# Mixer B's small matmuls in fewer lists: keys and values, outputs and output transposes each in one

## The chip, the core and the metric

One core of a Trainium2 chip runs the whole program. The metric is the device time of one execution in microseconds, median of three runs. On this core TensorE (PE) does the matmuls and transposes, with its weight loads (PEld) beside them; VectorE (DVE), ScalarE (ACT) and GpSimd (POOL) do the elementwise work; SyncE (SP) issues the transfers. Each engine takes its instructions strictly in the order of its own program, and waits on semaphores for the others.

## What is computed

Two layers over 1024 positions of width 1024, in fp32. Layer 0 mixes by dilated window attention, layer 1 by a gated linear recurrence (mixer B); behind each mixer stands a squared-ReLU MLP, and behind each of the four a residual sum with layer norm. The change lies in mixer B, with 8 heads of width 128 and chunks of 64 positions:

```python
q, key, log_f, v = chunks(q, K), chunks(key, K), chunks(log_f, K), chunks(v, V)
b = jnp.cumsum(log_f, axis=3)
q_dec = q * jnp.exp(b)
k_dec = key * jnp.exp(-b)
a = jnp.where(causal, jnp.einsum('bhcid,bhcjd->bhcij', q_dec, k_dec), 0.0)
o_intra = jnp.einsum('bhcij,bhcje->bhcie', a, v)
kv = jnp.einsum('bhcjd,bhcje->bhcde', key * jnp.exp(b_last - b), v)
def step(state, inp):
    dec, kv_c = inp
    return dec[..., None] * state + kv_c, state
_, states = lax.scan(step, s0, ...)
o_inter = jnp.einsum('bhcid,cbhde->bhcie', q_dec, states)
o = o_intra + o_inter
o = o * lax.rsqrt(jnp.mean(o * o, axis=-1, keepdims=True) + RMS_EPS) * norm_g
return o.reshape(B, S, H * V) @ w_out
```

## The kernel before

The kernel is written against a tile layer, which adds the semaphores and, within the limits that the code sets, puts each engine's instructions into an order at compile time. Every large matmul is three passes: fp32 operands are split into a high and a low part (`split`, L157 and L158; `wh`, `wl` for weights).

`hgrn` runs over 8 heads. A head has six **slots**, two halves of the positions for each of forget gate (t = 1), query (t = 0) and value (t = 2). Each slot projects with `proj` (L192 to L194, 24 matmuls of 128x512 into one of three PSUM banks "mm"), copies the bank with ScalarE (L1821), then takes one **list of pieces** from `pend` and runs it. Behind the slot in which both halves of a t are there stands that t's `gate` (L1765 to L1797): a chain over 128x1024 elements on ScalarE, VectorE and, for two additions (L1781 and L1795), GpSimd. The gates are those of the head being projected; the pieces are those of the head before, so both lie beside each other.

The pieces of a head come from `head_pieces`, which returns lists, one for each following slot:

- `trans` transposes values and keys on TensorE (L1677) into banks "pt"; ScalarE copies them (L1678) to `vn` and `k2n`.
- `amat(j)` makes the masked product of queries and keys of a half (L1685, banks "s"), and VectorE writes it to `aT` (L1687).
- `kv(j)` multiplies keys with values for eight (j = 0) or seven (j = 1) chunks (L1697, two banks), and VectorE steps the state through them (L1703, L1705): `stA` holds the states of the first half, `stB` of the second. A step reads the one before.
- `omat(j)` adds `aT` times values (L1718) and queries times states (L1723) into a bank, "o" for j = 0 and "s" for j = 1. Then the result is normalised: squares on ScalarE (L1726), a reduction (L1728) and small operations on VectorE (L1729 to L1735) with a logarithm and an exponential on ScalarE (L1730, L1731), and the scaled result `on` on VectorE (L1737).
- `otr(j)` transposes `on` (L1745), ScalarE copies it to `oN` with the norm's gain (L1746), and for heads 0 to 4 a transfer stores it.

A fp32 matmul of the pieces shows as two passes in the records, so `kv(0)` is 16 of them. Head 0's lists start one slot later. The last head's lists go to `outproj_ln`, whose `tick` counts its groups of three matmuls (L204 to L206) and hands out the lists evenly over 56 of them; what TensorE does there beside them is the output projection over the heads that are already done.

Of the kernel before, what the change touches and what calls it, by code (L numbers as in the profile page):

```python
# [69 lines left out]
def trunk_kernel(  # L70
# [32 lines left out]
    def U(name, dt=F32):  # L103
        return up.tile([P, 1024], dt, name=name, tag="u")

    def bank(tag, name):
        return ps.tile([P, 512], F32, name=name, tag=tag, bufs={"mm": 3, "s": 2, "pt": 2, "o": 1}[tag])

    def small(shape, name, bufs=4, dt=F32):
        return sp.tile(shape, dt, name=name, tag=name, bufs=bufs)  # L110
# [1548 lines left out]
    def hgrn(xs, late, consts, pre, gw):  # L1659
# [8 lines left out]
        def head_pieces(hd, kd, kd2, qd, vT, dec, oNt):  # L1668
            st = {}

            def trans(src, name):
                d = U(name)
                for j in range(2):
                    pt = bank("pt", "hpt")
                    for i in range(4):
                        b = j * 4 + i
                        nc.tensor.transpose(pt[:, i * P:(i + 1) * P], src[:, b * P:(b + 1) * P], ident)  # L1677
                    act(d[:, j * 512:(j + 1) * 512], pt, AF.Copy)  # L1678
                st[name] = d
# [9 lines left out]
            def kv(j):  # L1689
                if j == 0:  # L1690
                    st["S"] = [U("stA"), U("stB")]
                kb = [bank("s" if j else "pt", "kvps") for _ in range(2)]
                cs = [c for c in range(j * 8, j * 8 + 8) if c < NCH - 1]
                for c in cs:
                    r = slice((c % 2) * CH, (c % 2) * CH + CH)
                    t = c // 2
                    nc.tensor.matmul(kb[c % 2][:, (t % 4) * P:(t % 4 + 1) * P], st["k2n"][r, t * P:(t + 1) * P],  # L1697
                                     st["vn"][r, t * P:(t + 1) * P], start=True, stop=True, skip_group_check=True)
                for c in cs:
                    dst = state(c + 1)  # L1700
                    kvc = kb[c % 2][:, (c // 2 % 4) * P:(c // 2 % 4 + 1) * P]
                    if c == 0:
                        nc.vector.tensor_copy(dst, kvc)  # L1703
                    else:
                        nc.vector.scalar_tensor_tensor(dst, state(c), dec[:, c:c + 1], kvc,  # L1705
                                                       op0=ALU.mult, op1=ALU.add)

            def state(c):
                return st["S"][c // 8][:, (c % 8) * P:(c % 8 + 1) * P]

            def omat(j):
                o = bank("o" if j == 0 else "s", "ho")
                for i in range(4):
                    t = j * 4 + i
                    cs = slice(i * P, (i + 1) * P)
                    both = [(c, o[(c % 2) * CH:(c % 2) * CH + CH, cs]) for c in (2 * t, 2 * t + 1)]
                    for c, oc in both:
                        nc.tensor.matmul(oc, aTs[j][:, i * P + (c % 2) * CH:i * P + (c % 2) * CH + CH],  # L1718
                                         st["vn"][:, t * P:(t + 1) * P], start=True, stop=c == 0,
                                         skip_group_check=True)  # L1720
                    for c, oc in both:
                        if c:
                            nc.tensor.matmul(oc, qd[:, c * CH:(c + 1) * CH], state(c), start=False, stop=True,  # L1723
                                             skip_group_check=True)
                sq = wp.tile([P, 512], F32, name="sq", tag="p")
                act(sq, o, AF.Square)  # L1726
                w = small([P, 4, 4], "rms")
                nc.vector.tensor_reduce(w[:, 0], sq.rearrange("p (t e) -> p t e", e=P), axis=AX.X, op=ALU.add)  # L1728
                nc.vector.tensor_scalar(w[:, 0], w[:, 0], 1.0 / P, RMS_EPS, op0=ALU.mult, op1=ALU.add)  # L1729
                act(w[:, 1], w[:, 0], AF.Ln)  # L1730
                act(w[:, 1], w[:, 1], AF.Exp, scale=-0.5)  # L1731
                nc.vector.tensor_mul(w[:, 2], w[:, 0], w[:, 1])
                nc.vector.tensor_mul(w[:, 2], w[:, 2], w[:, 1])
                nc.vector.tensor_scalar(w[:, 2], w[:, 2], -0.5, 1.5, op0=ALU.mult, op1=ALU.add)
                nc.vector.tensor_mul(w[:, 3], w[:, 2], w[:, 1])  # L1735
                on = wp.tile([P, 512], F32, name="on", tag="pts", bufs=4)
                nc.vector.tensor_mul(on.rearrange("p (t e) -> p t e", e=P), o.rearrange("p (t e) -> p t e", e=P),  # L1737
                                     w[:, 3].unsqueeze(2).broadcast_to([P, 4, P]))
                st["on", j] = on

            def otr(j):
                on = st.pop(("on", j))
                pt = bank("o" if j else "pt", "opt")
                for i in range(4):
                    nc.tensor.transpose(pt[:, i * P:(i + 1) * P], on[:, i * P:(i + 1) * P], ident)  # L1745
                act(oNt[:, j * 512:(j + 1) * 512], pt, AF.Identity, scale=gT[:, hd:hd + 1])  # L1746
                if hd < SPILL[1] and j == 1:
                    nc.sync.dma_start(ond[1, hd], oNt)
# [2 lines left out]
            keys = lambda: trans(kd2, "k2n")  # L1751
            return [
                [lambda: trans(vT, "vn")] + (amats + [keys] if hd else [keys] + amats),
                [lambda: kv(0)],
                [lambda: omat(0), lambda: kv(1)],
                [lambda: omat(1)],
                [],
                [lambda: otr(0)],
                [lambda: otr(1)],
            ]  # L1760

        def gate(hd, t, e, cur, c):
# [40 lines left out]
        for hd in range(8):  # L1803
# [29 lines left out]
            oNt = U("oN")  # L1833
            oN.append(ond[1, hd] if hd < SPILL[1] else oNt)
            new = head_pieces(hd, cur["kd"], cur["kd2"], cur["qd"], e[2], cur["dec"], oNt)
            if hd == 0:
                new = [[]] + new
# [109 lines left out]
```

## Time and profile before

| | us |
|---|---|
| median of three runs | 2760.66 (2760.09 to 2762.2) |
| the profiled execution | 2761.49 |
| its span, first to last instruction | 2759.7 |
| stage of mixer B's projections | 1688 to 2035 |
| period of one head there (kv(0) to kv(0)) | 43.80 |

The profile is of one execution. Rows of a timeline are start in us, duration, engine, line, operation, output<-inputs, shapes and count, and in brackets how long the engine was idle before and what ended that. Matmuls overlap in the pipeline, so a duration is longer than the time to the next start; the starts tell what a matmul costs. A row of a stretch has its length, then busy time and count of TensorE, its weight loads, VectorE, ScalarE and GpSimd, the granted clock of TensorE (1.00 is full), the share of the DMA engines and GB/s. A row of waits has total, count and longest.

### The profile page before, as it was taken

The page shows a single profiled execution, that of the slowest core. Times are in us where ns is not written, and L with a number is a line of the kernel's source. Part 1 is how long each engine was busy: PE and PEld are TensorE (multiplying, and loading weights), DVE is VectorE, ACT ScalarE, POOL GpSimd, SP SyncE. Part 2 cuts the span into 40 slices and gives each one's busy share as a digit, 9 for nine tenths or more (in the row PEclk, how much of TensorE's full clock was granted, in tenths as well). Part 3 has the DMA queues.
Part 4 walks back from the last instruction along what each step waited for, and adds up shares of the span by engine and source line. Part 5 has one row for each costly group of instructions (what it writes and reads, how often), then busy time and mean ns, then how long its engine had stood idle before and what let it go on. Part 6 is the DMA issues. An engine that isn't in the chain of part 4 may idle for free.

```text
span 2759.7 us, 40110 instructions
## 1 busy us (share of the span) xinstructions
PE 2734.4 (99%) x14312; PEld 2237.2 (81%) x14312; DVE 2076.6 (75%) x3876; ACT 1419.4 (51%) x3059; POOL 69.0 (2%) x46
## 2 busy tenths in 40 slices
PE   9999999999999999999999999999999999999998
PEld 7888888888888777888888888888888888888887
DVE  8868877777888768876696777565678887678687
ACT  5555555555555456445454435455552545455443
POOL 0000000000000001000000000010100100000000
PEclk9999999999999999999999999999999999999999
DMA  8767666766767324454584852001142464485654
GB/s 303 257 209 214 197 205 191 234 185 212 225 208 226 120 94 160 168 211 152 186 290 134 275 171 92 31 32 62 65 130 104 149 220 170 143 292 191 217 176 129
DMA packets 204041, 485.02 MB, mean 176 GB/s; under 512 B 28992, under 2 KB 42816, under 8 KB 203840
## 3 DMA queue, kind: packets, MB, share of 16 engines
q1 hardware_dynamic: 203072, 482.19, 52.6%
q8 instruction: 113, 1.85, 0.3%
q14 instruction: 88, 0.72, 0.1%
q10 hardware_dynamic: 768, 0.26, 0.0%
HBM read 362.69 MB, written 94.11 MB: 166 GB/s over the span
## 4 chain that ended last, share of the span: by engine, by line
PE 92%; DVE 5%; ACT 1%; issue 1%; DMA 1%; SPq 0%; POOL 0%; DVEq 0%; ACTq 0%; POOLq 0%
PE pmm L752 8%; PE pmm L750 8%; PE pmm L751 8%; PE pup L1272 7%; PE pup L1270 7%; PE pup L1271 7%; PE pdy L1421 4%; PE pdy L1425 4%; PE pdy L1424 4%; PE pdx L1424 3%; PE pdx L1425 3%; PE pdx L1421 3%; PE pmm L192 3%; PE pmm L194 3%; PE pmm L193 3%; PE s L559 3%
## 5 line engine op out<-in xcount | busy, mean ns | idle before, releaser
L750 PE MATMUL pmm<-xh,H 128*128 128x512 f32 x1008 | 402.1, 399 | 2.0 <-ACT H L487 1.9
L752 PE MATMUL pmm<-xh,H 128*128 128x512 f32 x1008 | 394.0, 391 | 2.3 <-DVE H L495 2.2
L751 PE MATMUL pmm<-xl,H 128*128 128x512 f32 x1008 | 393.0, 390 | 0.7 <-DVE xl L158 0.7
L752 PEld LDWEIGHTS pmm<-xh,H 128*128 128x128 f32 x1008 | 189.2, 188 | 44.9 <-DVE H L495 4.3
L750 PEld LDWEIGHTS pmm<-xh,H 128*128 128x128 f32 x1008 | 189.5, 188 | 40.4 <-ACT H L487 3.0
L751 PEld LDWEIGHTS pmm<-xl,H 128*128 128x128 f32 x1008 | 189.7, 188 | 37.7 <-DVE xl L158 1.1
L575 ACT ACTIVATE p<-p,stats 128x128 f32<-128x128 f32 (+1 forms) x384 | 167.9, 440 | 81.6 <-DVE stats L572 81.4
L1421 PE MATMUL pdy<-dT,dS 128*128 128x512 f32 x512 | 199.2, 389 | 0.0
L1424 PE MATMUL pdy<-dT,dS 128*128 128x512 f32 x512 | 199.2, 389 | 0.0
L1425 PE MATMUL pdy<-dT,dS 128*128 128x512 f32 x512 | 199.2, 389 | 0.0
L572 DVE CUSTOM_DVE_ANT_0 p<-s,mask 128x128 f32<-128x128 f32 (+1 forms) x384 | 111.1, 348 | 98.9 <-PE s L559 91.0
L157 ACT ACTIVATE dS<-dr 128x512 fp32r<-128x512 f32 x192 | 119.4, 622 | 69.9 <-PE pdy L1425 36.2
L192 PE MATMUL pmm<-f0nh,wh 128*128 128x512 f32 x384 | 153.2, 399 | 0.0
L194 PE MATMUL pmm<-f0nh,wl 128*128 128x512 f32 x384 | 149.8, 390 | 0.0
L193 PE MATMUL pmm<-f0nl,wh 128*128 128x512 f32 x384 | 149.7, 390 | 0.0
L158 DVE TENSOR_TENSOR dS<-dr,dS 128x512 fp32r<-128x512 f32 x192 | 131.5, 685 | 7.6 <-ACT dS L157 7.6
L157 ACT ACTIVATE dT<-hold 128x512 fp32r<-128x512 f32 x128 | 80.1, 626 | 78.5 <-DVE hold L1400 33.4
L1231 ACT ACTIVATE H<-wc 128x512 fp32r<-128x512 f32 x128 | 77.2, 626 | 77.6 <-DVE wc L1224 46.4
L1425 PEld LDWEIGHTS pdy<-dT,dS 128*128 128x128 f32 x512 | 96.1, 188 | 20.1
L1424 PEld LDWEIGHTS pdy<-dT,dS 128*128 128x128 f32 x512 | 96.1, 188 | 19.9
L1421 PEld LDWEIGHTS pdy<-dT,dS 128*128 128x128 f32 x512 | 96.1, 188 | 19.8
L587 ACT ACTIVATE pts<-ppt 128x512 f32<-128x512 f32 (+1 forms) x146 | 77.7, 575 | 44.4 <-PE ppt L584 44.1
(412 smaller groups left out, 6836.0 us busy)
## 6 DMA issues: line engine op xcount, KB each, us to landing
xh<-xtd SPq DMA_DIRECT2D x110, 512.0 KB
xl<-xtd SPq DMA_DIRECT2D x110, 512.0 KB
dr<-hd SPq DMA_DIRECT2D x192, 256.0 KB
dr<-in_w_down_dram SPq DMA_DIRECT2D x128, 256.0 KB
rot<-e SPq DMA_DIRECT2D x192, 128.0 KB
wa<-in_w_up_dram SPq DMA_DIRECT2D x48, 512.0 KB
wb<-in_w_attn_dram SPq DMA_DIRECT2D x36, 512.0 KB
wa<-in_w_attn_dram SPq DMA_DIRECT2D x33, 512.0 KB
```

Source lines behind the costliest of these rows:

```text
L157: act(hi, raw, AF.Copy)
L192: nc.tensor.matmul(o, wh[:, k], xs.h(k), start=k == 0, stop=False)
L193: nc.tensor.matmul(o, wh[:, k], xs.l(k), start=False, stop=False)
L194: nc.tensor.matmul(o, wl[:, k], xs.h(k), start=False, stop=k == NK - 1)
L750: nc.tensor.matmul(o, wh, hi[k // 2][:, c], start=begin and k == 0, stop=False, skip_group_check=True)
L751: nc.tensor.matmul(o, wh, lo[k // 2][:, c], start=False, stop=False, skip_group_check=True)
L752: nc.tensor.matmul(o, wl, hi[k // 2][:, c], start=False, stop=end and k == 3, skip_group_check=True)
L1270: nc.tensor.matmul(o, wh, xf.h(b, k), start=begin and k == 0, stop=False, skip_group_check=True)
L1271: nc.tensor.matmul(o, wh, xf.l(b, k), start=False, stop=False, skip_group_check=True)
L1421: nc.tensor.matmul(o[q], h, T_[:, L], start=begin, stop=False, skip_group_check=True)
L1424: nc.tensor.matmul(o[q], h, T_[:, R], start=False, stop=False, skip_group_check=True)
L1425: nc.tensor.matmul(o[q], l, T_[:, L], start=False, stop=end, skip_group_check=True)
```

## The change

```diff
@@ -1751,12 +1751,11 @@
             keys = lambda: trans(kd2, "k2n")
             return [
                 [lambda: trans(vT, "vn")] + (amats + [keys] if hd else [keys] + amats),
-                [lambda: kv(0)],
-                [lambda: omat(0), lambda: kv(1)],
-                [lambda: omat(1)],
+                [lambda: kv(0), lambda: kv(1)],
                 [],
-                [lambda: otr(0)],
-                [lambda: otr(1)],
+                [lambda: omat(0), lambda: omat(1)],
+                [],
+                [lambda: otr(0), lambda: otr(1)],
             ]
```

Seven lists become six. `kv(1)` moves up one slot, `omat(0)` moves down one, `otr(1)` moves up one; `otr(0)`, `omat(1)` and `kv(0)` stay. Between `omat(1)` and `otr(1)` lie two slots instead of three, between `omat(0)` and `otr(0)` too. No instruction is added or removed. The order of SP's instructions is the same, and GpSimd's; on the other engines it differs only from the first head's pieces to the last head's. In the changed kernel each line behind the lists has a number lower by one.

In heads 1 to 5 TensorE's order follows the lists: 15 matmuls of kv in one row, two projections, 31 of omat in one row, two projections, eight output transposes, one projection, then the next head's transposes and masked products. Three places where the scheduler decides:

VectorE, a middle head, from the state steps to the first result, before (`kvps` are kv's banks, `stA` and `stB` the states, `ls` and `ze` the gate's tiles, a_ its scratch, `rms` the small tile of the normalisation, `sq` the squares):

```order
L1703 COPY stA<-kvps 128x128
L1705 SCALAR_TENSOR_TENSOR stA<-stA,dec,kvps 128x128 x6
L1705 SCALAR_TENSOR_TENSOR stB<-stA,dec,kvps 128x128
L1772 SCALAR_TENSOR_TENSOR ls<-ze,a_17383 128x1024
L1773 SCALAR_TENSOR_TENSOR ze<-ze,a_17383 128x1024
L1728 TENSOR_REDUCE rms<-sq 128x4
L1705 SCALAR_TENSOR_TENSOR stB<-stB,dec,kvps 128x128
```

and now:

```order
L1703 COPY stA<-kvps 128x128
L1705 SCALAR_TENSOR_TENSOR stA<-stA,dec,kvps 128x128 x6
L1705 SCALAR_TENSOR_TENSOR stB<-stA,dec,kvps 128x128
L1705 SCALAR_TENSOR_TENSOR stB<-stB,dec,kvps 128x128 x7
L1771 SCALAR_TENSOR_TENSOR ls<-ze,a_17399 128x1024
L1772 SCALAR_TENSOR_TENSOR ze<-ze,a_17399 128x1024
L1776 TENSOR_SCALAR ls<-ls,hc_C,hc_A 128x1024
L158 TENSOR_TENSOR wl<-wr,wh 128x1024
L1777 TENSOR_TENSOR ls<-ls,a_17399 128x1024
L1778 SCALAR_TENSOR_TENSOR a_17399<-smask,ls 128x1024
L1728 TENSOR_REDUCE rms<-sq 128x4
```

All state steps now stand ahead of the gate, and the first reduction of the outputs behind the gate's scan (L1779 before, L1778 now).

VectorE, a middle head, from the first result `on` to the second (`ho` is omat's bank, `qe` the query, `wl` the low part of a weight), before:

```order
L1737 TENSOR_TENSOR on<-ho,rms 128x512
L1784 TENSOR_TENSOR ze<-a_17032,ze 128x1024
L1728 TENSOR_REDUCE rms<-sq 128x4
L1794 SCALAR_TENSOR_TENSOR a_17185<-qe,a_17185 128x1024
L1729 TENSOR_SCALAR rms<-rms 128x4
L158 TENSOR_TENSOR wl<-wr,wh 128x1024
L1732 TENSOR_TENSOR rms<-rms 128x4
L1733 TENSOR_TENSOR rms<-rms 128x4
L1734 TENSOR_SCALAR rms<-rms 128x4
L1735 TENSOR_TENSOR rms<-rms 128x4
L1797 TENSOR_TENSOR qe<-qe,a_17185 128x1024
L1737 TENSOR_TENSOR on<-ho,rms 128x512
```

and now, from ahead of the first result to the second (ahead of these rows stand L1793, L1783, L1732 and L1728):

```order
L1733 TENSOR_TENSOR rms<-rms 128x4
L158 TENSOR_TENSOR wl<-wr,wh 128x1024
L1734 TENSOR_SCALAR rms<-rms 128x4
L1729 TENSOR_SCALAR rms<-rms 128x4
L1735 TENSOR_TENSOR rms<-rms 128x4
L1737 TENSOR_TENSOR on<-ho,rms 128x512
L1796 TENSOR_TENSOR qe<-qe,a_17536 128x1024
L1732 TENSOR_TENSOR rms<-rms 128x4
L1733 TENSOR_TENSOR rms<-rms 128x4
L1734 TENSOR_SCALAR rms<-rms 128x4
L1735 TENSOR_TENSOR rms<-rms 128x4
L1737 TENSOR_TENSOR on<-ho,rms 128x512
```

Before, the first result was done ahead of the gate's L1784, and of the second half only L1737 stood behind the query's last product L1797. Now both results come behind the gate (L1783), and the second half's small operations and its `on` behind the query's last product (L1796 now).

TensorE, head 7's pieces in the output projection (`hpt` are banks for transposes, `ho` omat's bank, `pmm` the output projection's), before:

```order
L1677 MATMUL hpt<-ident,ze 128x128 x4
L1718 MATMUL ho<-vn,aT 64x128
L1677 MATMUL hpt<-ident,ze 128x128 x4
L1697 MATMUL kvps<-vn,k2n 128x128 x8
L1718 MATMUL ho<-vn,aT 64x128
L1723 MATMUL ho<-stA,qe 64x128
L1718 MATMUL ho<-vn,aT 64x128 x2
L1697 MATMUL kvps<-vn,k2n 128x128 x3
L1723 MATMUL ho<-stA,qe 64x128
L1697 MATMUL kvps<-vn,k2n 128x128
L1723 MATMUL ho<-stA,qe 64x128
```

and now:

```order
L206 MATMUL pmm<-woh,hol 128x512
L1677 MATMUL hpt<-ident,ze 128x128 x4
L204 MATMUL pmm<-woh,hoh 128x512
L1677 MATMUL hpt<-ident,ze 128x128 x4
L1697 MATMUL kvps<-vn,k2n 128x128 x15
L205 MATMUL pmm<-wol,hoh 128x512
L206 MATMUL pmm<-woh,hol 128x512
L204 MATMUL pmm<-woh,hoh 128x512
```

Before, kv(1) and omat(0) stood mixed, 13 groups of the two in turn, and 15 matmuls of the output projection stood ahead of omat(1). Now all of kv stands together, 23 matmuls of the output projection follow it, then all of omat, and 54 further matmuls later both output transposes.

## The prediction

> **What bounds the kernel now.** I read the page first: its busy times, then the chain that ended last.
>
> ```profile
> PE 2734.4 (99%) x14312; PEld 2237.2 (81%) x14312; DVE 2076.6 (75%) x3876; ACT 1419.4 (51%) x3059; POOL 69.0 (2%) x46
> ...
> PE 92%; DVE 5%; ACT 1%; issue 1%; DMA 1%; SPq 0%; POOL 0%; DVEq 0%; ACTq 0%; POOLq 0%
> ```
>
> TensorE is the bound everywhere. A change pays only by making its stream of instructions shorter, and costs only where TensorE begins to wait. So I look at the stage of mixer B alone, first by stretches, then by what TensorE waited for from 1680 to 2180 us.
>
> ```profile
> 1688.00:2035.00 347.00, 346.52 (x2123) 288.42 (x2121) 216.71 (x334) 194.18 (x289) 38.74 (x18) 1.00 0.18 62
> ```
>
> ```profile
> PE pmm L206 <- DVE hol L158: 0.5, 1, 0.5
> PE ho L1718 <- DVE stB L1705: 0.2, 1, 0.2
> ```
>
> TensorE (the second number) is idle for half a microsecond of 347. No wait is left to remove, so the gain has to come from the matmuls themselves. For that I read TensorE's timeline, here for one head: the projection matmuls L192 to L194 and the small pieces between them.
>
> ```profile
> 1826.52 0.39 PE L194 MATMUL pmm<-f0nh,wl 128*128 128x512 f32 x1
> 1826.84 1.16 PE L1697 MATMUL kvps<-vn,k2n 64*128 64x128 f32 x16
> 1827.93 0.50 PE L192 MATMUL pmm<-f0nh,wh 128*128 128x512 f32 x1
> 1828.27 0.39 PE L193 MATMUL pmm<-f0nl,wh 128*128 128x512 f32 x1
> ...
> 1833.28 0.39 PE L194 MATMUL pmm<-f0nh,wl 128*128 128x512 f32 x1
> 1833.60 0.33 PE L1718 MATMUL ho<-vn,aT 128*64 128x128 f32 x2
> ...
> 1835.49 1.16 PE L1697 MATMUL kvps<-vn,k2n 64*128 64x128 f32 x14
> 1836.58 0.50 PE L192 MATMUL pmm<-f0nh,wh 128*128 128x512 f32 x1
> 1836.91 0.39 PE L193 MATMUL pmm<-f0nl,wh 128*128 128x512 f32 x1
> ...
> 1841.93 0.39 PE L194 MATMUL pmm<-f0nh,wl 128*128 128x512 f32 x1
> 1842.25 0.33 PE L1718 MATMUL ho<-vn,aT 128*64 128x128 f32 x2
> ...
> 1844.15 0.50 PE L192 MATMUL pmm<-f0nh,wh 128*128 128x512 f32 x1
> 1844.48 0.40 PE L193 MATMUL pmm<-f0nl,wh 128*128 128x512 f32 x1
> ```
>
> From 1828.27 to 1833.28 lie 22 steps: 0.227 us for a projection matmul, 5.44 us for a list's 24. Each change between the shapes 128\*128, 64\*128 and 128\*64 makes the next step longer: 0.32 into a piece, 0.34 for the second projection matmul behind one. So a list's pieces cost the time from the last projection matmul to the second one after them, less two steps: kv(0) 1.75 - 0.45 = 1.30, omat(0) with kv(1) 3.63 - 0.45 = 3.18, omat(1) 2.55 - 0.45 = 2.10; together 6.58 us.
>
> **The gain: fewer changes of shape.** Inside a group the steps are short. The 16 passes of kv(0) run in pairs: (1.16 - 0.27) / 8 = 0.11 us a pair; omat(1)'s 16 pairs take 1842.25 to 1844.15, entry and exit included, so about 0.11 each too. kv(1) directly behind kv(0) is eight steps, 0.88 us, instead of 1835.49 to 1836.58, 1.09: it saves 0.20. omat(1) directly behind omat(0) is 16 steps, 1.76, instead of 2.10: it saves 0.34. That is 0.54 us a head, and 3.8 us in heads 0 to 6. In head 0 there is a little more: the wait of 0.2 us quoted above for stB falls away, with a slow restart behind it; I take 0.4.
>
> The output transposes keep the projections' shape, and gain nothing.
>
> ```profile
> 1811.37 0.60 PE L1745 MATMUL opt<-ident,on 128*128 128x128 f32 x4
> ```
>
> Four of them are 0.60 us of overlapping records, and no change of shape stands ahead of them or behind them.
>
> Head 7's pieces lie in the output projection. Before, the scheduler had mixed omat(0) with the keys' transposes and kv(1), as the order rows on this place show.
>
> ```profile
> 2048.84 0.40 PE L206 MATMUL pmm<-woh,hol 128*128 128x512 f32 x1
> 2049.07 0.60 PE L1677 MATMUL hpt<-ident,ze 128*128 128x128 f32 x4
> ...
> 2057.75 0.50 PE L204 MATMUL pmm<-woh,hoh 128*128 128x512 f32 x1
> 2058.08 0.40 PE L205 MATMUL pmm<-wol,hoh 128*128 128x512 f32 x1
> ```
>
> That stretch costs 9.24 - 0.45 = 8.79 us, and omat(1) by itself 2.10 as above: 10.89. After the change the rows are separate: eight transposes 0.88, kv 1.30 + 0.88 = 2.18, omat 2.10 + 1.76 = 3.86, together 6.92. This saves 4.0 us. The gain in all: 3.8 + 0.4 + 4.0 = **8.2 us**. What stands behind omat here is 54 projection matmuls, 12.2 us, before the transposes, so I expect no new wait in head 7.
>
> **The cost: the transposes come sooner after omat.** Before, both transposes ran three lists after their omat; now two, so only two projections (10.9 us) lie between. In that time ScalarE and VectorE must normalise both halves, beside the gates of the next head. The rows that set this, VectorE's, ScalarE's and GpSimd's timelines of the same head:
>
> ```profile
> 1828.03 0.29 DVE L1703 COPY stA<-kvps 128x128 f32<-128x128 f32 x1 [6.72 <-PE kvps L1697]
> 1828.42 2.26 DVE L1705 SCALAR_TENSOR_TENSOR stA<-stA,dec,kvps 128x128 f32<-128x128 f32 x6
> 1830.72 0.35 DVE L1705 SCALAR_TENSOR_TENSOR stB<-stA,dec,kvps 128x128 f32<-128x128 f32 x1
> 1830.99 1.22 DVE L1772 SCALAR_TENSOR_TENSOR ls<-ze,a 128x1024 f32<-128x1024 f32 x1
> ...
> 1842.16 2.29 DVE L1779 TENSOR_TENSOR_SCAN a<-smask,ls 128x1024 f32<-128x1024 f32 x1
> ...
> 1848.22 1.23 DVE L1784 TENSOR_TENSOR ze<-a,ze 128x1024 f32<-128x1024 f32 x1 [0.47 <-ACT ls L1782]
> ...
> 1851.73 3.06 DVE L158 TENSOR_TENSOR wl<-wr,wh 128x1024 fp32r<-128x1024 f32 x1 [0.47 <-ACT wh L157]
> ...
> 1855.37 1.22 DVE L1797 TENSOR_TENSOR qe<-qe,a 128x1024 f32<-128x1024 f32 x1
> 1856.51 0.68 DVE L1737 TENSOR_TENSOR on<-ho,rms 128x512 f32<-128x512 f32 x1
> ```
>
> ```profile
> 1836.10 1.14 ACT L1774 ACTIVATE a<-ls,hc_CA 128x1024 f32<-128x1024 f32 x1
> ...
> 1839.51 1.14 ACT L1776 ACTIVATE a<-a,one 128x1024 f32<-128x1024 f32 x1
> ```
>
> ```profile
> 1844.59 2.41 POOL L1781 TENSOR_TENSOR ze<-ze,a 128x1024 f32<-128x1024 f32 x1 [34.60 <-DVE rms L1733]
> 1851.31 2.39 POOL L1795 TENSOR_TENSOR a<-a,a 128x1024 f32<-128x1024 f32 x1 [4.31 <-DVE rms L1729]
> ```
>
> I lay out a head after the change from its first kv matmul (time 0). VectorE now does all 15 state steps before it turns to the gate: first copy at 1.19, first step 1.58, then 0.383 each, so L1772 starts at 6.83 and L1773 (I take L1772's 1.22) ends at 9.3. ScalarE from L1774 to L1776's end is 4.55: 13.9. L1778 (again 1.22) ends at 15.15, L1779 at 17.5, GpSimd's L1781 at **X = 20.0**.
>
> Here two things meet. L158's usual 1.2 us became 3.06 because it stood beside GpSimd's L1795: it ended 1.09 after L1795 did. I take it that every VectorE operation with two operands in SBUF is held so. Now L1794 stands beside L1781 (it is free some 1.2 us before X) and ends at X + 1.09, which starts GpSimd's L1795 at X + 1.2; and L1784, which waits for ScalarE's L1782, is ready at X + 1.22 (1848.22 against 1847.00 above). It is held until L1795 ends, and is done at X + 1.2 + 2.4 + 1.09 = X + 4.7. If L1784 wins that tie, the small operation behind it is held instead, and the end is the same within 0.2.
>
> Then the order rows put on VectorE, ahead of the second half's result: a reduction (0.6, an estimate by L1737, which has as many elements), a weight split (1.13: L1772's 1.22 less the overlap of neighbours), small operations of the first half (0.6), its L1737 (0.6), L1797 (1.14), four small operations (0.6) and L1737 (0.69): 5.3 us. The second "on" is ready at 20.0 + 4.7 + 5.3 = 30.05. TensorE is at the second transposes at: kv 1.98 + 0.11, two projections 10.88, omat 3.85, two projections 10.88 and four transposes 0.44, which makes 28.15. So it **waits 1.9 to 2.0 us a head**; the first "on" is ready at 27.5, just in time for 27.7. This holds for heads 1 to 5. Head 6 has no weight split in the row: 1.13 less, 0.8 us. Head 0 has another order, and no wait. Waits: 5 x 1.95 + 0.8 = 10.5 us. Behind the waiting transposes stands the next head's first projection, and ScalarE's copy and the next gate wait for that: all of it moves along. The order of SP's queue is the same; only the store of a finished head is issued a list earlier, and nobody reads it before the output projection. Bounds for a head's wait: nothing, if none of VectorE's operations is held (rival 1), and 3.4 us, if each of the chain's some 25 steps begins 0.06 us later than I laid them.
>
> **A second price: the clock.** Three stretches of one length, near 1060 us (the number behind POOL's is the granted clock):
>
> ```profile
> 1059.79:1063.20 3.41, 1.78 (x12) 1.26 (x12) 3.41 (x7) 2.78 (x6) 0.61 (x1) 1.00 0.95 353
> 1063.20:1066.62 3.42, 1.48 (x5) 0.59 (x4) 3.35 (x6) 1.74 (x5) 0.68 (x1) 1.00 1.00 379
> 1066.62:1070.03 3.41, 3.24 (x8) 2.56 (x9) 3.16 (x7) 0.00 (x0) 0.00 (x0) 0.50 0.08 31
> ```
>
> After 1.48 us of work in 3.42 the clock was halved for 3.41 us; after 1.78 it was not. A wait of 1.95 leaves 1.46, if it falls within one such stretch. By chance of phase that is about half of the five heads; each costs 3.41 / 2 = 1.7 us. I take two: 3.4 us.
>
> The Trainium skill (TensorE: Matmul & The Clock Gate, section What's actually happening) has the clock fall after an idle window of about 3.4 us; by that rule a wait of 2 us never lowers it. The row above, with 1.48 us of work in the stretch, speaks against it, and I follow the row.
>
> **The sum.** Against the profiled execution, 2761.49 us: - 8.2 + 10.5 + 3.4 = + 5.7, so 2767.2. That execution lies 0.8 above the median of 2760.66; against the median the forecast is **2766 us**, slower by 0.2%, which is about what a measurement of this kernel can tell from no change.
>
> **Rivals.** (1) *No wait, faster.* If GpSimd's additions hold neither L1794 nor L1784, L1784 ends at X + 2.45 and the last result at X + 7.7 = 27.7, before TensorE is there (28.15 is the point from which it decides). Then only the gain is left: 2760.7 - 8.2 = 2752.5. For it: the whole chain is a sum of some 25 steps, and 2 us off is 7%. Against it: L158's row. (2) *L1794 is not held* (no row of this head has it beside GpSimd), L1784 is: all is 1.1 earlier, the wait 0.85 in five heads, and the clock stays: 2760.7 - 8.2 + 4.3 = 2756.8. (3) *The wait comes as worked out, and the clock never falls*: 2760.7 - 8.2 + 10.5 = 2763.0. This is the page's rule; for it speaks that one place of the trace is a thin base. (4) *The clock falls in all five heads*: 2763.0 + 8.5 = 2771.5; a longer wait makes that likelier.
>
> **Chances and range.** Forecast 0.38 (one to three falls of the clock, 2764.7 to 2768.1), rival 1 0.17, rival 2 0.18, rival 3 0.20, rival 4 0.07. The range 2752 to 2770 takes in the first three rivals; the bounds of the wait (0 and 3.4 us) ask for it. Faster by more than 0.2% (below 2755.1) is rival 1 and a little of rival 2: 0.20. Slower (above 2766.2) is rival 4 and most of the forecast: 0.36. The rest, 0.44, is within 0.2%.
>
> **What would show it.** In TensorE's timeline of a middle head: kv as one group of about 2.2 us, omat as one of 3.9, no other shape between. Among TensorE's waits: a row of L1744 (L1745 before) for VectorE's "on", some six times, about 2 us each; no such row speaks for rival 1. On VectorE: L1783 (L1784 before) 3.5 us long beside GpSimd. Among the stretches: a granted clock below 1 between 1780 and 2035 us, or none. Head 7's stretch from its second set of keys' transposes without a change between omat and kv. The prediction is wrong if TensorE waits elsewhere, at omat or at the keys' transposes, or if the output projection waits for the last head's transposes.

## The result, and the profile after

| | before | changed |
|---|---|---|
| median, us | 2761.69 (6 runs) | 2772.23 (2770.77 to 2773.76, 6 runs) |
| ratio | | 1.0039 (95% interval 1.0028 to 1.005) |
| profiled execution / its span, us | 2761.49 / 2759.7 | 2770.77 / 2768.7 |

The change costs 10.5 us. The forecast was 5.7 over the profiled execution, and the result lies outside the range. The page of the changed kernel, busy times and the chain that ended last:

```profile
PE 2733.0 (99%) x14312; PEld 2239.7 (81%) x14312; DVE 2079.8 (75%) x3876; ACT 1419.0 (51%) x3059; POOL 76.0 (3%) x46
...
PE 87%; DVE 8%; ACT 2%; issue 1%; DMA 1%; POOL 0%; SPq 0%; DVEq 0%; ACTq 0%; POOLq 0%
```

TensorE has as much work as before, and VectorE a larger part in the chain. The stretch of mixer B from 1688 us to the end of the last head's transposes, and what TensorE waited for from 1680 to 2180 us:

```profile
1688.00:2046.00 358.00, 346.31 (x2113) 289.45 (x2112) 218.66 (x332) 193.66 (x289) 45.78 (x18) 0.99 0.17 57
```

```profile
PE opt L1745 <- DVE on L1737: 11.6, 8, 2.0
PE pmm L206 <- DVE hol L158: 0.5, 1, 0.5
```

Before, TensorE was idle for half a microsecond here; now it is idle for 11.7 of 358, all but a little of it in front of the output transposes, and the mean granted clock is 0.99. TensorE's timeline of one head shows gain and loss side by side:

```profile
1920.37 0.39 PE L194 MATMUL pmm<-f0nh,wl 128*128 128x512 f32 x1
1920.69 2.05 PE L1697 MATMUL kvps<-vn,k2n 64*128 64x128 f32 x30
1922.67 0.50 PE L192 MATMUL pmm<-f0nh,wh 128*128 128x512 f32 x1
1923.01 0.39 PE L193 MATMUL pmm<-f0nl,wh 128*128 128x512 f32 x1
...
1933.46 0.39 PE L194 MATMUL pmm<-f0nh,wl 128*128 128x512 f32 x1
...
1937.42 0.50 PE L192 MATMUL pmm<-f0nh,wh 128*128 128x512 f32 x1
1937.76 0.40 PE L193 MATMUL pmm<-f0nl,wh 128*128 128x512 f32 x1
...
1948.20 0.39 PE L194 MATMUL pmm<-f0nh,wl 128*128 128x512 f32 x1
1948.52 0.66 PE L1745 MATMUL opt<-ident,on 128*128 128x128 f32 x4
1951.21 0.63 PE L1745 MATMUL opt<-ident,on 128*128 128x128 f32 x4 [2.03 <-DVE on L1737]
1951.59 0.48 PE L192 MATMUL pmm<-f0nh,wh 128*128 128x512 f32 x1
1951.91 0.40 PE L193 MATMUL pmm<-f0nl,wh 128*128 128x512 f32 x1
```

Counted as in the prediction (from the last projection matmul to the second one behind, less two steps), kv costs 2.64 - 0.45 = 2.19 and omat 4.30 - 0.45 = 3.85. The eight transposes cost 3.71 - 0.45 = 3.26, where two groups of four cost 0.89 before. Over all heads, counted in this way from the starts in the trace:

| part, us | forecast | trace of the changed kernel |
|---|---|---|
| gain, heads 1 to 6 | -3.2 | -3.3 |
| gain, head 0 | -0.9 | -1.3 |
| gain, last head's pieces | -4.0 | -3.4 |
| wait, heads 1 to 5 | +9.75 | +12.4 |
| the same, head 6 | +0.8 | +1.55 |
| clock | +3.4 (two falls) | +4.7 (three falls) |
| sum | +5.7 | +10.6 |

The medians differ by 10.5. The two profiled executions differ by 9.3, and 1.3 of what is missing lies ahead of mixer B, which this execution reached 1.3 us earlier. From head 0's first transposes to the first transposes of the next layer norm the changed trace is 10.1 us longer (382.4 against 372.2), so the parts together are good to half a microsecond.

Why the wait is as long as it is, VectorE's and GpSimd's timelines of the same head show (L1783 here is L1784 of before, and so on):

```profile
1938.24 0.66 DVE L1728 TENSOR_REDUCE rms<-sq 128x4 f32<-128x512 f32 x1
1938.94 1.95 DVE L1729 TENSOR_SCALAR rms<-rms 128x4 f32<-128x4 f32 x1
1940.80 1.21 DVE L1793 SCALAR_TENSOR_TENSOR a<-qe,a 128x1024 f32<-128x1024 f32 x1
1942.08 1.23 DVE L1783 TENSOR_TENSOR ze<-a,ze 128x1024 f32<-128x1024 f32 x1
1943.23 2.36 DVE L1732 TENSOR_TENSOR rms<-rms 128x4 f32<-128x4 f32 x1
...
1947.77 0.69 DVE L1737 TENSOR_TENSOR on<-ho,rms 128x512 f32<-128x512 f32 x1
...
1950.37 0.69 DVE L1737 TENSOR_TENSOR on<-ho,rms 128x512 f32<-128x512 f32 x1
```

```profile
1938.46 2.40 POOL L1780 TENSOR_TENSOR ze<-ze,a 128x1024 f32<-128x1024 f32 x1 [40.08 <-DVE a L1778]
1942.15 3.42 POOL L1794 TENSOR_TENSOR a<-a,a 128x1024 f32<-128x1024 f32 x1 [1.29 <-DVE a L1793]
```

L1729 and L1732, operations on 128x4 numbers that take 0.15 us elsewhere, last until GpSimd's additions end (1938.46 + 2.40 = 1940.86, 1942.15 + 3.42 = 1945.57). From the first kv matmul at 1920.69 the second "on" is ready after 30.37 us. TensorE, at 0.11 us a transpose, would be at the second four after 28.27; it began at 30.52: a wait of 2.25, of which the row counts 2.03, since it begins at the modelled end of the transposes before.

Last, the clock. Two stretches, each with the one behind it (TensorE's work is the second number, the granted clock the third from the end):

```profile
1853.94:1857.35 3.41, 1.38 (x10) 1.13 (x11) 2.24 (x6) 1.43 (x3) 0.00 (x0) 1.00 0.00 0
1857.35:1860.76 3.41, 3.41 (x10) 2.66 (x9) 1.23 (x1) 1.48 (x2) 0.00 (x0) 0.50 0.61 187
1949.51:1952.92 3.41, 1.71 (x10) 1.52 (x11) 1.34 (x6) 1.44 (x3) 0.00 (x0) 1.00 0.02 5
1952.92:1956.33 3.41, 3.41 (x17) 2.80 (x16) 1.22 (x1) 0.59 (x1) 0.00 (x0) 1.00 0.84 271
```

After the first, with 1.38 us of work, the clock was halved for 3.41 us; after the other, with 1.71, it was not. Two more halved stretches of mixer B begin at 1905.14 and 1997.30.

### The profile page after: what moved, and what is told of

Same layout as the page of the kernel before. It is cut to its first block, busy times and chain, and to the rows that moved or that the text cites. A ratio compares the mean times of both kernels' runs of the same rounds, so it can differ in the third digit from the quotient of the medians.

```text
span 2768.7 us, 40142 instructions
## 1 busy us (share of the span) xinstructions
PE 2733.0 (99%) x14312; PEld 2239.7 (81%) x14312; DVE 2079.8 (75%) x3876; ACT 1419.0 (51%) x3059; POOL 76.0 (3%) x46
## 3 DMA queue, kind: packets, MB, share of 16 engines
q8 instruction: 113, 1.85, 0.3%
## 4 chain that ended last, share of the span: by engine, by line
PE 87%; DVE 8%; ACT 2%; issue 1%; DMA 1%; POOL 0%; SPq 0%; DVEq 0%; ACTq 0%; POOLq 0%
PE pmm L752 8%; PE pmm L750 8%; PE pmm L751 8%; PE pup L1272 7%; PE pup L1270 7%; PE pup L1271 7%; PE pdy L1425 4%; PE pdy L1424 4%; PE pdy L1421 4%; PE pdx L1424 3%; PE pdx L1425 3%; PE pdx L1421 3%; PE s L559 3%; PE ppt L584 2%; PE o L598 2%; PE pmm L206 2%
## 5 line engine op out<-in xcount | busy, mean ns | idle before, releaser
L158 DVE TENSOR_TENSOR dS<-dr,dS 128x512 fp32r<-128x512 f32 x192 | 131.7, 686 | 7.4 <-ACT dS L157 7.4
```

## The experiments

The theory: gluing saves 8 us, as forecast; the loss is TensorE's wait for the second "on", made long by GpSimd's two additions, and the falls of the clock behind it. The rivals: gluing itself delays VectorE; the chain is too long without any holding; the falls have another cause. The experiments that were timed beside each other share their runs of before; "before" was 2761.6 to 2762.0 us in all of them.

**The second transposes one list later.** In the changed kernel:

```diff
-                [lambda: otr(0), lambda: otr(1)],
+                [lambda: otr(0)],
+                [lambda: otr(1)],
```

> The change with one part undone: the second output transposes stay one list (a projection, 5.4 us) behind the first, as before; keys and values together and outputs together stay. Theory: the gluing of kv and omat saves 7 to 8 us and the loss comes only from the second transposes' wait for their VectorE operand (about 2.2 us a head) and the clock's falls behind it. Then no wait for that operand is left among TensorE's waits, the granted clock stays at 1 from 1750 to 2035 us, and the time is 7 to 8 us below before: about 2754. Rival: the gluing itself delays VectorE and costs what it saves; then the time is within 2 us of before or above it.

Measured: 2757.01 us, ratio 0.9983 (0.9974 to 0.9992): faster than before by 4.9, so the gain exists and the rival falls. But the theory wanted 7 to 8 and no wait. TensorE's waits from 1680 to 2180 us of this kernel:

```profile
PE opt L1745 <- DVE on L1737: 1.4, 3, 0.9
```

Head 6, in whose place the scheduler still put all eight transposes in one row, pays 1.55 us as in the changed kernel, and in heads 1 to 5 the first transposes come 0.1 to 0.5 late: 1.1 together. 8.0 - 2.65 = 5.3, near the 4.9.

**Only the transposes together.** In the kernel before:

```diff
-                [lambda: otr(0)],
-                [lambda: otr(1)],
+                [lambda: otr(0), lambda: otr(1)],
```

> The kernel before with only one part of the change: both output transposes in the list in which the first stood (a list earlier than before for the second); keys and values and outputs apart, as before. Theory: the wait belongs to the short way from the second omat to the second transposes, which is two projections here too: a row of waits for VectorE's second half of 1 to 2 us a head, and without the gain of the gluing 2766 to 2773. Rival: the glued kv makes the wait, since its 15 state steps in one block push the gate's chain back; then here hardly a wait is left, and the time is that of before, 2760 to 2763.

Measured: 2770.17 us, ratio 1.0032 (1.002 to 1.0044). The wait is there without any gluing; its row, and two stretches:

```profile
PE opt L1745 <- DVE on L1737: 7.8, 5, 1.8
```

```profile
1809.55:1812.96 3.41, 1.85 (x13) 1.47 (x12) 2.07 (x4) 1.71 (x3) 0.00 (x0) 1.00 0.00 0
1812.96:1816.37 3.41, 3.41 (x17) 2.80 (x16) 1.23 (x1) 1.10 (x2) 0.00 (x0) 1.00 0.71 234
```

The eight transposes of heads 1 to 5 cost 8.9 us more than before, and that is all of the 8.6. With 1.7 to 2.0 us a head instead of 2.4 to 2.7, and at least 1.85 us of work in each such stretch, the clock never fell. So the short way from omat to its transposes makes the wait; gluing makes it some 0.7 us a head longer.

**Only keys and values together.** In the kernel before:

```diff
-                [lambda: kv(0)],
-                [lambda: omat(0), lambda: kv(1)],
+                [lambda: kv(0), lambda: kv(1)],
+                [lambda: omat(0)],
```

> The kernel before with only keys and values together: kv(0) and kv(1) in one list, both omats and both output transposes in lists of their own as before. Theory: it saves 0.20 us a head by one change of shape less, some 1 us in head 0, and 2 to 3 us in the last head's pieces, which stand less mixed; no wait, since three projections lie between the second omat and its transposes: 2756 to 2759. Rival: the 15 state steps in one block delay VectorE by enough that the transposes wait here too, or an omat waits for the states: a row of such waits, and 2761 or more.

Measured: 2758.71 us, ratio 0.9989 (0.9981 to 0.9998), faster by 3.2. kv with both omats costs 2.18 + 2.10 + 2.10 = 6.38 a head, 0.20 less than before, as forecast. Hardly a wait: 0.3 us in all by the row, at head 6's transposes, which the scheduler put into one row of eight here too; by the starts they cost 0.8 more than before.

**Both additions on VectorE.** In the changed kernel:

```diff
-                nc.gpsimd.tensor_add(z, z, a1)
+                nc.vector.tensor_add(z, z, a1)
...
-                nc.gpsimd.tensor_add(a3, a3, cur["a"][:, c])
+                nc.vector.tensor_add(a3, a3, cur["a"][:, c])
```

> The changed kernel, with both additions of the gates on VectorE instead of GpSimd, so that nothing runs beside VectorE. Theory: the wait comes from VectorE operations that are held while GpSimd adds. Each addition then takes about 1.2 us instead of 2.4 to 3.4, the second operand is ready near 28 us after the first kv matmul instead of 30.5, and TensorE's wait for it falls from 2.2 us to 0.5 at most, without falls of the clock: about 2755. Rival: the chain is too long by its own length, not by the holding; VectorE gains 1.2 us on the first addition and loses 1.2 by the second: the wait stays at about 2 us a head and the time at 2770 to 2773.

Measured: 2755.52 us, ratio 0.9978 (0.9969 to 0.9987): 6.4 faster than before, 16.7 faster than the changed kernel, and no row of a wait for "on". VectorE's timeline of the same head:

```profile
1929.61 1.21 DVE L1780 TENSOR_TENSOR ze<-ze,a 128x1024 f32<-128x1024 f32 x1
1930.74 0.16 DVE L1729 TENSOR_SCALAR rms<-rms 128x4 f32<-128x4 f32 x1
...
1932.54 1.21 DVE L1783 TENSOR_TENSOR ze<-a,ze 128x1024 f32<-128x1024 f32 x1
1933.67 0.15 DVE L1732 TENSOR_TENSOR rms<-rms 128x4 f32<-128x4 f32 x1
```

VectorE does more work and is done sooner: L1729 takes 0.16 instead of 1.95, L1732 0.15 instead of 2.36. The second "on" is ready 27.98 us after the first kv matmul instead of 30.37, and the eight transposes cost 0.89 again. From head 0's first transposes to the second eight transposes of the next layer norm the kernel is 7.9 us shorter than before (375.1 against 383.0), close to the forecast gain of 8.2. From there to the end the profiled execution is about 1.9 us longer than before's; the next feed-forward waits 1.1 us for ScalarE there; whether every execution gives it back stays open.

**The same in the kernel before.** Both additions on VectorE, nothing else:

> The kernel before with both of the gates' additions on VectorE, as in the run that took the wait away. Theory: before has no wait there, so moving the additions brings nothing by itself, and the 6.4 us by which the changed kernel with additions on VectorE beats before are the gain of the gluing: 2760 to 2763. Rival: the moved additions are themselves worth some us, and the gluing less: 2758 or below.

Measured: 2761.86 us, ratio 0.9998 (0.9989 to 1.0007). Before, the additions' place is worth nothing that these runs can tell from noise.

**Each addition alone.** In the changed kernel, first the one on ze, then the one on a:

> The changed kernel with the first of the gates' two additions (on ze) on VectorE, the second (on a) still on GpSimd. With both on VectorE the wait was gone (2755.5). Theory: each addition holds VectorE once, some 2 us, so that taking away one leaves a wait of 0.7 to 1.9 us a head: 2758 to 2768. Rival A: the first addition alone makes the wait (it delays the chain itself, and holds the small operation behind it): no wait left, 2755 to 2757. Rival B: the second alone makes it: 2770 to 2773.

> The changed kernel with the second of the gates' two additions on VectorE, the first still on GpSimd. Theory (each holds once): VectorE's small operation is still held by the first addition for 1.9 us, nothing is held behind it: the wait is about 1.3 us a head, 2758 to 2766. Rival A (the first alone makes the wait): 2770 to 2773. Rival B (the second alone): no wait left, 2755 to 2757.

Measured: 2757.77 us, ratio 0.9985 (0.9976 to 0.9994), and 2758.79 us, ratio 0.9987 (0.9979 to 0.9996). Each addition holds once, as the theory has it, though the first time lies 0.2 below the range that I expected. With the first on VectorE (VectorE's and GpSimd's rows):

```profile
1935.88 3.10 DVE L1783 TENSOR_TENSOR ze<-a,ze 128x1024 f32<-128x1024 f32 x1
1938.90 0.15 DVE L1732 TENSOR_TENSOR rms<-rms 128x4 f32<-128x4 f32 x1
```

```profile
1935.50 2.39 POOL L1794 TENSOR_TENSOR a<-a,a 128x1024 f32<-128x1024 f32 x1 [41.57 <-issue]
```

Here GpSimd starts first, takes its 2.39, and L1783 is held behind it; with both on VectorE L1783 took 1.21. With the second on VectorE, L1729 is held behind the first addition still:

```profile
1931.09 1.95 DVE L1729 TENSOR_SCALAR rms<-rms 128x4 f32<-128x4 f32 x1
```

Either way the transposes cost 0.8 to 1.1 us a head more than without a wait, under half of the changed kernel's 2.4 to 2.7. With the second on VectorE the profile puts most of the wait down to ScalarE's copy L1746; the second "on" was done 0.08 us before that copy ended (1941.87 and 1941.95), so the row can't say which of the two TensorE waited for.

**The wait filled.** In the changed kernel, 16 transposes of the identity matrix ahead of the second output transposes of heads 1 to 5, and 4 in another kernel; what they write is overwritten:

```diff
+                if j and 1 <= hd <= 5:
+                    for i in range(16):
+                        nc.tensor.transpose(pt[:, i % 4 * P:(i % 4 + 1) * P], ident, ident)
```

> The changed kernel, with 16 further transposes of the identity matrix on TensorE (into the bank that the second output transposes then overwrite) ahead of the second output transposes of heads 1 to 5: about 1.8 us of idle work inside the wait. Theory: some 4.7 us of the loss are three falls of the clock, caused by little work in a 3.4-us stretch. With the wait filled the end of the wait stays where it is, the clock stays at 1 from 1750 to 2035 us, and the time is 4 to 6 us below the changed kernel: about 2767. Rival: the falls have another cause, or cost nothing beside the wait: the time stays at 2771 to 2774, or goes up.

> The changed kernel with only 4 identity transposes instead of 16 ahead of the second output transposes of heads 1 to 5: about 0.45 us of TensorE work inside the wait. In the traces so far the granted clock is set anew every 3.41 us; three stretches of the changed kernel with 1.38 us of work were followed by half the clock, as was before's with 1.48, while those with 1.72 (the changed kernel) and 1.86 to 2.12 (the kernel with only the transposes together) were not. Theory: the share of work in one such stretch decides, at a point between 1.48 and 1.72 of 3.41 us. Then 0.45 us more, 1.8 in all, is enough: no fall between 1750 and 2035 us, and the time is that of 16 transposes, 2766 to 2768. Rival: the length of the wait decides; it is still 1.7 to 1.8 us at a stretch, so at least two falls stay, and 2769 to 2773.

> The changed kernel itself, beside the two others on the same chip, for a comparison with the filled waits: 2771 to 2774, with waits of about 2 us in five heads and two to four falls of the clock.

Measured: 2767.17 us with 16, ratio 1.0021 (1.0012 to 1.003); 2767.67 us with 4, ratio 1.0021 (1.0012 to 1.003); the changed kernel again 2771.69 us, ratio 1.0037 (1.0024 to 1.0049). Useless work makes the kernel 4 to 5 us faster, and a quarter of it is enough. The waiting transposes of heads 1 to 5 still cost 11.9 us more than without a wait in both kernels, against 12.4 unfilled, so nearly all that was won is the clock: from 1750 to 2035 us it is 1.00 in both, against 0.98 unfilled. With 4 the emptiest stretch, where TensorE still waits 1.5 us in one piece, and the one behind it:

```profile
1809.31:1812.72 3.41, 1.90 (x14) 1.24 (x13) 2.83 (x7) 1.62 (x4) 0.00 (x0) 1.00 0.00 0
1812.72:1816.13 3.41, 3.41 (x19) 2.81 (x17) 1.23 (x1) 1.63 (x2) 0.00 (x0) 1.00 0.46 154
```

The rival, that the length of the wait decides, had asked for a wait of 1.7 to 1.8 us here, and it was 1.5, so this run alone doesn't settle it. Before's fall at 1066.62, whose rows the prediction shows, does: TensorE's longest wait there was 1.37 us, and behind the longer 1.5 us here no fall came.

The changed kernel's second profile had four falls in mixer B, three after 1.38 us and one after 1.44; a stretch with 1.56 was followed by none:

```profile
1808.56:1811.97 3.41, 1.44 (x8) 0.74 (x6) 3.08 (x7) 1.91 (x5) 0.00 (x0) 1.00 0.00 0
1811.97:1815.38 3.41, 3.35 (x10) 2.90 (x11) 0.56 (x1) 1.63 (x2) 0.00 (x0) 0.50 0.21 85
1951.92:1955.33 3.41, 1.56 (x9) 1.40 (x10) 1.50 (x6) 1.44 (x3) 0.00 (x0) 1.00 0.02 5
1955.33:1958.74 3.41, 3.41 (x17) 2.81 (x16) 1.23 (x1) 0.74 (x1) 0.00 (x0) 1.00 0.85 262
```

**The outputs one list earlier.** In the changed kernel, three projections between omat and the transposes, but one between kv and omat:

```diff
                 [lambda: kv(0), lambda: kv(1)],
-                [],
                 [lambda: omat(0), lambda: omat(1)],
+                [],
                 [],
```

> The lists of the change with both halves of the outputs one list earlier: one projection between kv and omat, three between omat and both output transposes. Theory: the second normalised half is ready some 25 us after the first kv matmul, the transposes come at 27.6, so no wait and no fall of the clock, and the gain of the gluing is kept but for some mixing in the last head's pieces: 6 to 8 us below before, about 2755. Rival: omat now waits for the last state steps of VectorE, or the next head's score matrices for the gate that has moved behind the normalisation: then a row of such a wait of 1 us or more a head, and 2760 or more.

Measured: 2765.1 us, ratio 1.0012 (1.0003 to 1.0021): slower than before, and my expectation of 2755 missed. No wait for "on" is left, but three others came; then the stretch of head 0 and the two behind it:

```profile
PE ho L1718 <- DVE stB L1705: 3.2, 1, 3.2
PE as L1685 <- DVE qe L1796: 1.6, 1, 1.6
PE pmm L194 <- DVE wl L158: 1.4, 5, 0.3
```

```profile
1754.38:1757.79 3.41, 1.12 (x4) 0.60 (x4) 1.88 (x4) 2.56 (x3) 0.78 (x1) 1.00 0.00 0
1757.79:1761.20 3.41, 2.52 (x24) 2.52 (x26) 1.97 (x6) 3.41 (x5) 0.00 (x0) 0.50 0.02 5
1761.20:1764.61 3.41, 3.41 (x18) 2.60 (x15) 2.47 (x5) 1.95 (x5) 0.00 (x0) 0.50 0.00 0
```

In head 0 the state steps wait behind the gate, and omat for them, with two halved stretches behind it; at the last head the masked products wait for the gate that now stands behind the normalisation; and a weight split comes late in five heads. I had worked out only the middle heads.

## Why the prediction was wrong

The chain, the holding beside GpSimd and the place of the wait were right. Which operations are held was not, and the sizes of the wait and of the clock's loss were too small.

- **The gain** held: 8.0 against 8.2. kv and omat cost 2.18 and 3.85 a head, to the hundredth as worked out. Head 0 gave 0.4 more. The last head's pieces gave 0.6 less, most of it a pause inside its kv, whose row is 0.45 longer than the 2.05 of a middle head:

```profile
2062.68 2.50 PE L1697 MATMUL kvps<-vn,k2n 64*128 64x128 f32 x30
```

- **"Waits 1.9 to 2.0 us a head"** is the term that was mis-sized most. The sum held L1794 and L1784 (L1793 and L1783 now). Neither was held: they took 1.21 and 1.23 us, and the 3.5 us of L1783 that the prediction named as a sign did not come. Held were the 128x4 operations L1729, ahead of L1793, and L1732, behind L1783. For the second the prediction had this as the other way to the same end (L1784 wins the tie), and the end came at X + 4.73 instead of X + 4.7. X itself came at 20.17 instead of 20.0, the rest of the chain was some 0.15 longer, the transposes began 0.15 behind the result, and TensorE itself was 0.12 later, which takes that much off: 2.25 instead of 1.9. What the sum left out are the first transposes: the first "on" is ready at 27.77, not 27.5, and they start 0.1 to 0.4 us late. In all 2.4 to 2.7 a head. In a chain of 30 us, 1% of its length is a sixth of the wait.
- **"Head 6 ... 0.8 us"** was half of it. I took one weight split out of the row; the trace shows a wait at each of its two halves, 1.16 us of idle rows and 1.55 by the starts. Its second "on" came 29.56 us after its first kv matmul, only 0.81 before a middle head's, not 1.13:

```profile
2041.53 0.66 PE L1745 MATMUL opt<-ident,on 128*128 128x128 f32 x4 [0.26 <-DVE on L1737]
2043.09 0.63 PE L1745 MATMUL opt<-ident,on 128*128 128x128 f32 x4 [0.90 <-DVE on L1737]
```

- **"I take two"** falls of the clock: there were three, and four in the second profile. The row from 1060 us was a good base. Filling the wait shows that the falls come from the empty part of the stretch, and by the starts each of the three falls cost 1.4 to 1.6 us, near the 1.7 of the forecast. The longer wait made them likelier: at 1.7 to 2.0 us a head (only the transposes together) none of five fell. The Trainium skill (TensorE: Matmul & The Clock Gate, section What's actually happening) has a free-running window of 3413 ns, and the trace agrees: the falls at 1857.35, 1905.14 and 1997.30 lie 14 and 27 such windows apart. That a window must be idle for a fall, as that section also has it, the runs contradict: windows with 1.38 and 1.44 us of work were followed by one.
- **Rival 1** (no wait) and **rival 2** (one operation not held) are refuted in the changed kernel, but each became true where its condition was made: without GpSimd's additions no wait, with one of them about 1 us. The forecast's condition, that VectorE is held beside GpSimd, is what the pair of kernels with the additions on VectorE shows.
- **The range** ended at 2770, under the case with five falls, although that case and a longer wait go together; the bound of 3.4 us a head stood in the text, and the range left it out. One microsecond of the miss is the base: before's median was 2760.66 of three runs and is 2761.69 of six.

What beats both kernels: the changed lists with both additions on VectorE, 2755.52 us. The kernel with only the second transposes moved back, 2757.01, and the one with the first addition moved, 2757.77, are hardly told apart from it.

## What to carry to other kernels

Gluing small matmuls of one shape pays what the trace says a change of shape costs (0.2 to 0.34 us here), but a consumer that comes one list earlier must be checked against the end of the chain on the other engines, at the first and last rounds as well as in the middle. A wait on a TensorE that is otherwise full can cost more than its length: half a clock for 3.41 us when too little of one such stretch was work. Moving work off a busy VectorE onto GpSimd can make VectorE's chain longer; look for tiny operations that end when GpSimd's ends.

## What the runs showed of the hardware

- While GpSimd's addition of two SBUF tiles ran, VectorE's small operations of the normalisation lasted until its end, even one of 128x4 with a single input (L1729: 1.95 to 2.31 us instead of 0.16), and a weight split (L158) ended 1.09 us behind it. Operations that read a bank of PSUM were not held: beside L1780 the state steps (L1705) took 0.35 us each as elsewhere, and beside L1795 of the kernel with only keys and values together L1737 took its 0.69. Where VectorE's operation began first, GpSimd was the one that waited: L1794 took 3.42 beside L1783's 1.23, and 2.39 where it began first, with L1783 held for 3.10. The Trainium skill (SBUF — State Buffer, section Who interferes with whom) says that "Issue order, not op shape, decides who blocks"; as to who waits, these rows agree.
- The granted clock is set anew for whole stretches of 3.41 us. In mixer B it was halved after stretches with 1.12 (the outputs one list earlier), 1.38 and 1.44 us of work and not after 1.56, 1.71 and more; before had a fall after 1.48. Elsewhere no such point shows: it fell after 1.62 near 1067 us with only keys and values together and after 1.69 in the rows below, and after 1.84 near 27 us with both additions on VectorE, but not after 1.63 near 1069 us with the second addition on VectorE. So the busy time of a stretch is not the whole rule, and what else decides stays open. With the first addition on VectorE:

```profile
1064.64:1068.05 3.41, 1.69 (x6) 0.97 (x6) 3.34 (x6) 1.53 (x4) 0.00 (x0) 1.00 0.82 328
1068.05:1071.47 3.42, 3.42 (x9) 2.67 (x8) 2.21 (x5) 0.17 (x1) 0.00 (x0) 0.50 0.08 32
```

- A halved stretch with only 2.52 us of work (the outputs one list earlier, 1757.79) was followed by another halved one; behind halved stretches with 3.24 us of work and more the clock was full again.
